# HGRN mixer of a hybrid encoder layer: 64-wide corner products with full 128-column weights, first in the bank, then the 32-wide products of both directions as one group

## The chip, the cores and the metric

The kernel runs on one core of one Trainium2 chip. The metric is the time of one execution on the device in microseconds (us); lower is better. Times given are medians of several executions; a profile is one further execution.

## The reference

One layer of a bidirectional encoder, run on two sequences of 512 and 1024 tokens (12 tiles of 128 tokens, 3 blocks of 512), width 1024, all f32. Each layer norms its input, projects it, and runs two token mixers side by side: a Gated DeltaNet (GDN, 4 heads) and an HGRN2 (4 heads, key and value width 128), each forward and backward. Their outputs are gated, merged and projected, and a SwiGLU feed-forward follows. The part that the change touches is the HGRN2 recurrence, per head and direction:

```
S_t = diag(f_t) S_{t-1} + k_t v_t^T      k_t = 1 - f_t      o_t = S_t^T q_t
cum    = cumsum(logf)                    # inside a chunk
attn   = where(causal, (q * exp(cum)) @ (k * exp(-cum))^T, 0)
o      = attn @ v + (q * exp(cum)) @ S   # S carried from chunk to chunk
S_next = S * exp(cum_last) + (k * exp(cum_last - cum))^T @ v
```

The backward direction is the same on the flipped sequence, and both outputs are added, so one 128 x 128 matrix of scores per tile can hold the forward direction on one side of the diagonal and the backward direction on the other.

## The kernel before, in words

The kernel takes chunks of 128 tokens for the HGRN2. exp(cum) and exp(-cum) over 128 tokens would overflow, so the 128 x 128 scores of a tile are cut by distance from the diagonal, each piece with its own reference point for cum. For one head, one block of 512 tokens (4 tiles, index t) and one direction d, these products are made, all with 128 partitions of contraction (the key width):

- 16 diagonal products of 32 x 32 (4 per tile), from `e1` (queries) and `e2` (keys); forward into the bank `pa`, backward into a second bank `pb`
- 8 products of 32 x 32 (2 per tile) that lie beside the diagonal blocks inside each half of 64, from `l32`
- 4 products of 64 x 64 (1 per tile), the corner between the two halves of 64, from `l64`; forward and backward fill opposite corners of `pa`

`level(w)` prepares `l32` and `l64`: two subtractions on POOL, an exponential on ACT, two multiplications on DVE. `hg_pre` runs this for one direction, then makes its products, transposes the decayed keys `kd` and multiplies them with the values into a state increment. `hg_attn` runs the two directions side by side for each block, then copies `pa` and `pb` out of PSUM under masks that drop what no direction needs, and `hg_mix` carries the state and forms the outputs. There are 4 heads x 3 blocks = 12 such blocks in the program.

All f32 matmuls here run as two passes on TensorE, each with its own weight load. Most of TensorE's work is something else: projections, whose operands are split into a high and a low fp32r part and whose passes move 512 columns (tiles `ha` and `wa`). The GDN mixer has narrow products of its own: merges of 32 x 32 and 64 x 64 pieces, with contraction 32 and 64.

Two planners set the order. `Plan.run` walks five generators (GDN, HGRN, prelude, projections, second phase) by their priority and by estimated times; a `yield pl.at(tile)` hands over until that tile is estimated ready. That gives a program order. `Tape.schedule` then places every instruction on its engine's queue, taking of the instructions that are estimated ready the one that comes first in program order. It adds an estimated 400 ns whenever TensorE goes from one narrow weight shape to another or back, and to keep these few, it ties products of one narrow shape that follow each other in the program into one unit, which is placed whole (`Tape.units`). A product with 128 x 128 weights has no such shape (`o.form` stays None) and is placed alone, between whatever else is ready:

```
                    o.occ = 2 * (2 * k / 2.4 + 5.5) if k > 32 else 35
                    if form != (P, P):
                        o.form = form
```

`k` is the number of moving columns. The estimates only set the order; the chip runs each engine's queue in that order with semaphores.

Of the kernel before, what the change touches and what calls it, by code (L numbers as in the profile page):

```python
# [20 lines left out]
P = 128  # L21
# [671 lines left out]
def layer(ctx, tc, x_p, x_s, w_in, conv_w, a_log, dt_bias, gdn_w, lb_logits, hg_w, w_bg, w_bh,  # L693
# [57 lines left out]
    def mm(out, lhsT, rhs, start=True, stop=True):  # L751
        nc.tensor.matmul(out, lhsT, rhs, start=start, stop=stop)
        n = pl.cols(rhs)
        pl.op("PE", out, [lhsT, rhs], n / 2400.0 if rhs.dtype == F32R else max(0.05, n / 600.0))
# [120 lines left out]
    def t4(ap):  # L875
        return ap.rearrange("p (t c) -> p t c", c=P)
# [125 lines left out]
    def par(*gens):  # L1002
        st = [[0.0, g] for g in gens]
        while st:
            s = min(st, key=lambda c: c[0])
            yield ("at", s[0])
            try:
                r = next(s[1])
            except StopIteration:
                st.remove(s)  # L1010
                continue
            while callable(r):
                yield r
                r = 0
            s[0] = pl.end if r is None else r[1] if isinstance(r, tuple) else 0.0
# [592 lines left out]
    def hg_attn(q, h):  # L1608
        out = q.hg[h]
        for b in range(q.nb):  # L1610
            pa = px()
            pb = px()
            yield from par(*[hg_pre(h, out, b, d, t4(pa), pb[:, 0:P].rearrange("p (t c) -> p t c", c=32))
                             for d in range(2)])
            a_ = ht_("pa", 2)
            av = t4(a_)
            pset(a_, 0.0)
            nc.vector.copy_predicated(av, m_all[:, None, :].to_broadcast([P, 4, P]), t4(pa))
            pl.op("DVE", a_, [pa, a_])
            bd = sblk("bd").rearrange("p (t c) -> p t c", c=32)  # L1620
            pset(bd, 0.0)
            nc.vector.copy_predicated(bd, m_b[:, None, :].to_broadcast([P, 4, 32]),
                                      pb[:, 0:P].rearrange("p (t c) -> p t c", c=32))
            pl.op("DVE", bd, [pb, bd])
            for j in range(4):
                sl = slice(32 * j, 32 * j + 32)
                tt(av[sl, :, sl], av[sl, :, sl], bd[sl], ALU.add)
            out["pa", b] = a_
            yield None

    def hg_pre(h, out, b, d, pav, pbv):
        q = out["q"][b]
        sf = out["sf%d" % d][b]
        vtok = out["v"][b]
        li = d * 4 + h
        lf = blk("lf")
        act(lf, sf, AF.Ln, scale=oml[:, li:li + 1], bias=lb[:, li:li + 1])
# [40 lines left out]
            tt(dm[:, :, q_z], qv[:, :, q_z], dm[:, :, q_z], ALU.mult)  # L1678
            return dl

        def level_mm(w, dl):
            for t in range(4):
                for j in range(P // (2 * w)):
                    o0 = 2 * j * w
                    ks = slice(o0 + k_z * w, o0 + k_z * w + w)
                    qs = slice(o0 + q_z * w, o0 + q_z * w + w)
                    mm(pav[ks, t, qs], t4(dl)[:, t, ks], t4(dl)[:, t, qs])

        l32 = level(32)
        yield pl.at(e1, e2)  # L1690
        for t in range(4):
            for j in range(4):
                sl = slice(32 * j, 32 * j + 32)
                fs = slice(t * P + 32 * j, t * P + 32 * j + 32)
                mm(pav[sl, t, sl] if d == 0 else pbv[sl, t, :], e2[:, fs], e1[:, fs])
        l64 = level(64)
        et = sp.tile([P, 4], F32, name="et", tag="et", bufs=8)
        qs_ = ht_("qd", 4)
        kd = blk("kd")
# [10 lines left out]
            act(t4(kd), c, AF.Exp)  # L1710
        tt(kd, kk, kd, ALU.mult)
        tt(qs_, q, qs_, ALU.mult)
        yield pl.at(l32)
        level_mm(32, l32)
        yield pl.at(l64)
        level_mm(64, l64)
        yield pl.at(kd)
        kdt = blk("kdt")
        transp(kdt, kd)
# [577 lines left out]
```

## Time and profile before

| | us |
|---|---|
| median of 3 runs | 2542.62 (2541.12 to 2545.33) |
| profiled execution | 2537.38 |
| its span, first to last instruction | 2535.7 |
| TensorE (PE) busy | 2481.3 (98%) |
| weight loads (PEld) busy | 2038.3 (80%) |
| VectorE (DVE) busy | 1726.6 (68%) |
| ScalarE (ACT) busy | 1298.2 (51%) |
| GpSimd (POOL) busy | 738.7 (29%) |

Nearly all instructions carry line 577, where the planned order is emitted, so groups are told apart by tiles and shapes. Names of tiles are those of arenas: `ha`, `wa` hold the split operands of projections, `la`, `ba` most f32 tiles of the mixers, `sa` constants such as the identity of a transpose, `bank` PSUM. In a row, `128*64 128x64` means weights of 128 partitions and 64 columns and a result form of 128 x 64; `x8` is the number of passes; a second number after the start is the length. The bracket at the end of a row is the idle time before it and what ended it. PEclk is the clock granted to TensorE, 1.00 being full. The HGRN products run between 116 and 1257 us of the span.

### The profile page before, as it was taken

Reading aid. Unit: us, or ns where it says so; the run is one execution under the profiler, and the core shown is the slowest. Engines: PE = TensorE matmul, PEld = TensorE weight load, DVE = VectorE, ACT = ScalarE, POOL = GpSimd, SP = SyncE. Lnnn points to the kernel's source line nnn. Section 1 sums busy time; section 2 is a strip of 40 time slices with the busy share of each in tenths; the row PEclk is TensorE's granted clock in tenths of the full one; section 3 lists DMA queues with packets and bytes.
Section 4 is the critical chain, followed back from the end, with each engine's and each line's share of the span. In section 5 each row is a group of like instructions: output and inputs, shape, how many; then the busy total and the mean of one; then the engine's idle time right before and its main releaser. Section 6 shows DMA issues by size and latency. Waiting matters only on the chain.

```text
span 2535.7 us, 37670 instructions
## 1 busy us (share of the span) xinstructions
PE 2481.3 (98%) x13992; PEld 2038.3 (80%) x13992; DVE 1726.6 (68%) x2863; ACT 1298.2 (51%) x2202; POOL 738.7 (29%) x1011
## 2 busy tenths in 40 slices
PE   7999999999999999999999999999999999999998
PEld 6778888887878878888888888878888888888886
DVE  5877788768776665775766565664787787734458
ACT  5756666655656555663645435443444344433333
POOL 1551604152322231140100002112567676200014
PEclk9999999999999999999999999999999999999999
DMA  6245352322330331240576553354355455484453
GB/s 160 69 119 134 83 151 72 106 46 64 96 92 22 88 83 30 60 137 30 183 237 224 179 178 112 116 169 140 98 178 187 155 194 187 146 286 127 152 184 137
DMA packets 387303, 330.38 MB, mean 130 GB/s; under 512 B 55241, under 2 KB 315935, under 8 KB 387119
## 3 DMA queue, kind: packets, MB, share of 16 engines
q1 hardware_dynamic: 387119, 327.97, 42.4%
q8 instruction: 110, 1.80, 0.3%
q14 instruction: 74, 0.61, 0.1%
HBM read 251.44 MB, written 76.46 MB: 129 GB/s over the span
## 4 chain that ended last, share of the span: by engine, by line
PE 83%; DVE 6%; DMA 3%; POOL 3%; ACT 2%; issue 2%; SPq 1%; DVEq 0%; POOLq 0%; ACTq 0%
PE bank L577 83%; DVE la_a L577 3%; DVE ba_a L577 2%; POOL sm_a L577 1%; ACT la_a L577 1%; SPq L577 1%; DMA la_a<-dram_cr_sc 1%; POOL ba_a L577 1%; DVE wa_a L577 1%; ACT ba_a L577 1%; POOL la_a L577 1%; DMA la_a<-dram_u_sc 0%; ACT wa_a L577 0%; DMA dram_a_sc<-ba_a 0%; DVE sm_a L577 0%
## 5 line engine op out<-in xcount | busy, mean ns | idle before, releaser
L577 PE MATMUL bank<-ha_a,wa_a 128*128 128x512 f32 x5496 | 1455.0, 405 | 3.6 <-DVE wa_a L577 2.3
L577 PEld LDWEIGHTS bank<-ha_a,wa_a 128*128 128x128 f32 x5496 | 1006.8, 189 | 192.7 <-DVE wa_a L577 7.9
L577 PE MATMUL bank<-xr_a,ha_a 128*128 128x512 f32 x1200 | 318.7, 395 | 0.0
L577 PE MATMUL bank<-xr_a 128*128 128x512 f32 x1386 | 315.7, 389 | 0.0
L577 PEld LDWEIGHTS bank<-xr_a 128*128 128x128 f32 x1386 | 260.1, 188 | 54.1
L577 PEld LDWEIGHTS bank<-xr_a,ha_a 128*128 128x128 f32 x1200 | 225.4, 188 | 53.9
L577 DVE TENSOR_TENSOR wa_a<-la_a,wa_a 128x1024 fp32r<-128x1024 f32 (+1 forms) x152 | 172.9, 1148 | 125.4 <-PE bank L577 94.5
L577 POOL TENSOR_TENSOR ba_a<-ba_a 128x512 f32<-128x512 f32 (+1 forms) x127 | 173.9, 1376 | 269.4 <-DVE ba_a L577 100.6
L577 ACT ACTIVATE la_a<-la_a 128x512 f32<-128x512 f32 (+1 forms) x290 | 182.4, 643 | 60.2 <-DVE la_a L577 41.6
L577 ACT ACTIVATE wa_a<-la_a 128x1024 fp32r<-128x1024 f32 (+1 forms) x152 | 146.3, 973 | 118.5 <-PE bank L577 109.5
L577 POOL TENSOR_TENSOR la_a<-la_a 128x256 f32<-128x256 f32 (+1 forms) x56 | 53.8, 976 | 452.5 <-DVE la_a L577 414.6
L577 ACT ACTIVATE ha_a<-ba_a 128x512 fp32r<-128x512 f32 x135 | 84.6, 629 | 160.1 <-PE bank L577 114.2
L577 ACT ACTIVATE wa_a<-ba_a 128x1024 fp32r<-128x1024 f32 (+1 forms) x106 | 96.7, 921 | 124.7 <-PE bank L577 115.3
L577 PE MATMUL bank<-ha_a 128*128 128x512 f32 x480 | 149.4, 392 | 0.0
L577 DVE TENSOR_TENSOR ha_a<-ba_a,ha_a 128x512 fp32r<-128x512 f32 x135 | 130.7, 972 | 21.9 <-ACT ha_a L577 21.6
L577 DVE TENSOR_TENSOR wa_a<-ba_a,wa_a 128x1024 fp32r<-128x1024 f32 (+1 forms) x106 | 117.2, 1114 | 39.8 <-PE bank L577 31.0
L577 PE MATMUL bank<-wa_a,ha_a 128*128 128x512 f32 x576 | 133.7, 389 | 1.9 <-DVE wa_a L577 1.9
L577 POOL TENSOR_TENSOR sm_a<-la_a 128x126 f32<-128x126 f32 (+37 forms) x155 | 76.3, 492 | 199.4 <-DMA la_a<-dram_u_sc 152.9
L577 DVE TENSOR_TENSOR xr_a<-da_a,xr_a 128x1024 fp32r<-128x1024 f32 (+2 forms) x68 | 77.6, 1157 | 74.5 <-ACT xr_a L577 52.1
L577 ACT ACTIVATE ba_a<-ba_a 128x512 f32<-128x512 f32 (+1 forms) x184 | 115.2, 634 | 25.3 <-DVE ba_a L577 14.0
L577 PEld LDWEIGHTS bank<-wa_a,ha_a 128*128 128x128 f32 x576 | 108.0, 188 | 24.7 <-DVE wa_a L577 2.4
L577 ACT ACTIVATE xr_a<-da_a 128x1024 fp32r<-128x1024 f32 (+2 forms) x68 | 65.3, 978 | 101.9 <-PE bank L577 83.8
(193 smaller groups left out, 3605.0 us busy)
## 6 DMA issues: line engine op xcount, KB each, us to landing
la_a<-w_in SPq DMA_DIRECT2D x77, 512.0 KB
ba_a<-w_ffn_gate SPq DMA_DIRECT2D x36, 512.0 KB
ba_a<-w_ffn_up SPq DMA_DIRECT2D x33, 512.0 KB
dram_a_sc<-xa_a SPq DMA_DIRECT2D x63, 256.0 KB
ba_a<-w_in SPq DMA_DIRECT2D x27, 512.0 KB
da_a<-dram_a_sc SPq DMA_DIRECT2D x25, 512.0 KB
ba_a<-w_ffn_down SPq DMA_DIRECT2D x22, 512.0 KB
la_a<-w_out SPq DMA_DIRECT2D x17, 512.0 KB
```

Source lines behind the costliest of these rows:

```text
L577: f(*[m(a) for a in o.args], **{k: m(a) for k, a in o.kw.items()})
```

## The change

The code of `hg_pre` that made products is moved to `hg_attn`, behind the preparation of both directions; what came after the products becomes `hg_post`. The order in a block is now:

1. prepare both directions: `e1`, `e2`, `l64`, then `l32`, `kd`, `qd`, and wait until all four level tiles are estimated ready
2. the corner products: the full 128 columns of `l64` of a tile as weights, 64 columns of it as moving operand, into all 128 partitions of that half of `pa`. Of each product one half of the partitions is the wanted corner; the other half is written with numbers that nobody needs, and is overwritten by step 3 or dropped by the mask
3. the 48 products of 32 columns of both directions in one stretch of the program
4. both directions' transposes and state increments (`hg_post`), then the masked copies as before

```diff
-            yield from par(*[hg_pre(h, out, b, d, t4(pa), pb[:, 0:P].rearrange("p (t c) -> p t c", c=32))
-                             for d in range(2)])
+            parts = [{}, {}]
+            yield from par(*[hg_pre(h, out, b, d, parts[d]) for d in range(2)])
+            pav, pbv = t4(pa), pb[:, 0:P].rearrange("p (t c) -> p t c", c=32)
+            halves = [slice(0, 64), slice(64, P)]
+            yield pl.at(parts[0]["l64"], parts[1]["l64"], parts[0]["l32"], parts[1]["l32"])
+            for d in range(2):
+                dl = t4(parts[d]["l64"])
+                for t in range(4):
+                    mm(pav[:, t, halves[1 - d]], dl[:, t, :], dl[:, t, halves[1 - d]])
+            for d in range(2):
+                e1, e2, l32 = [parts[d][n] for n in ("e1", "e2", "l32")]
+                for t in range(4):
+                    for j in range(4):
+                        sl = slice(32 * j, 32 * j + 32)
+                        fs = slice(t * P + 32 * j, t * P + 32 * j + 32)
+                        mm(pav[sl, t, sl] if d == 0 else pbv[sl, t, :], e2[:, fs], e1[:, fs])
+                    for j in (0, 2):
+                        ks, qs = [slice(32 * (j + z), 32 * (j + z) + 32) for z in (d, 1 - d)]
+                        mm(pav[ks, t, qs], t4(l32)[:, t, ks], t4(l32)[:, t, qs])
+            yield from par(*[hg_post(out, b, d, parts[d]) for d in range(2)])
...
-        def level_mm(w, dl):
-            for t in range(4):
-                for j in range(P // (2 * w)):
-                    o0 = 2 * j * w
-                    ks = slice(o0 + k_z * w, o0 + k_z * w + w)
-                    qs = slice(o0 + q_z * w, o0 + q_z * w + w)
-                    mm(pav[ks, t, qs], t4(dl)[:, t, ks], t4(dl)[:, t, qs])
-
+        l64 = level(64)
+        yield pl.at(e1, e2)
         l32 = level(32)
-        yield pl.at(e1, e2)
-        for t in range(4):
-            for j in range(4):
...
-        l64 = level(64)
+        yield 0
...
-        yield pl.at(l32)
-        level_mm(32, l32)
-        yield pl.at(l64)
-        level_mm(64, l64)
+        part.update(e1=e1, e2=e2, l32=l32, l64=l64, kd=kd, qs=qs_, et=et)
+
+    def hg_post(out, b, d, part):
+        vtok = out["v"][b]
+        kd, qs_, et = [part[n] for n in ("kd", "qs", "et")]
         yield pl.at(kd)
```

TensorE's queue shows the change at two places. The names are result bank, then arenas of the operands; the shape is that of the result. The first place is a later block, of the second sequence and its second head. Before, it reads:

```order
L577 MATMUL bank_90<-la_a,ba_a 32x32 x16
L577 MATMUL bank_90<-la_a 32x32 x8
L577 MATMUL bank_87<-la_a 32x32 x16
L577 MATMUL bank_90<-ba_a 32x32 x8
L577 MATMUL bank_89<-ha_a,wa_a 128x512
L577 MATMUL bank_91<-ha_a,wa_a 128x512
L577 MATMUL bank_89<-ha_a,wa_a 128x512 x2
L577 MATMUL bank_91<-ha_a,wa_a 128x512 x2
L577 MATMUL bank_90<-la_a 64x64 x4
L577 MATMUL bank_91<-ha_a,wa_a 128x512
L577 MATMUL bank_93<-sa_a,ba_a 128x128
L577 MATMUL bank_90<-la_a 64x64 x4
```

Now, from the end of the corner products on:

```order
L577 MATMUL bank_94<-la_a 128x64 x2
L577 MATMUL bank_90<-sa_a,la_a 128x128
L577 MATMUL bank_89<-sa_a,ba_a 128x128
L577 MATMUL bank_94<-la_a 128x64
L577 MATMUL bank_87<-ha_a,wa_a 128x512
L577 MATMUL bank_94<-la_a 128x64
L577 MATMUL bank_89<-sa_a,ba_a 128x128
L577 MATMUL bank_87<-ha_a,wa_a 128x512
L577 MATMUL bank_94<-la_a 128x64
L577 MATMUL bank_94<-la_a 32x32 x24
L577 MATMUL bank_88<-la_a 32x32 x4
L577 MATMUL bank_94<-la_a 32x32 x2
```

The two groups of four 64x64 products behind the 32-wide ones are gone; the corners (128x64) stand one by one ahead of the 48 products of 32x32, with transposes (sa) and projection passes between them.

The second place is the first block of the program, whose 32-wide products stood in two groups. Before:

```order
L577 MATMUL bank_94<-la_a 32x32 x24
L577 MATMUL bank_89<-ba_a,la_a 32x32 x16
L577 MATMUL bank_88<-ha_a,wa_a 128x512 x3
L577 MATMUL bank_93<-ha_a,wa_a 128x512
L577 MATMUL bank_88<-ha_a,wa_a 128x512
L577 MATMUL bank_93<-ha_a,wa_a 128x512
L577 MATMUL bank_88<-ha_a,wa_a 128x512 x2
L577 MATMUL bank_93<-ha_a,wa_a 128x512
L577 MATMUL bank_88<-ha_a,wa_a 128x512
L577 MATMUL bank_93<-ha_a,wa_a 128x512
L577 MATMUL bank_88<-ha_a,wa_a 128x512 x2
L577 MATMUL bank_94<-ba_a 32x32 x8
```

Now:

```order
L577 MATMUL bank_93<-ha_a,wa_a 128x512 x2
L577 MATMUL bank_94<-ba_a 128x64
L577 MATMUL bank_93<-ha_a,wa_a 128x512
L577 MATMUL bank_94<-ba_a 128x64
L577 MATMUL bank_93<-ha_a,wa_a 128x512 x5
L577 MATMUL bank_94<-la_a 32x32 x24
L577 MATMUL bank_89<-ba_a,la_a 32x32 x4
L577 MATMUL bank_94<-ba_a 32x32 x2
```

The two groups of 40 and 8 products of 32x32 became one of 48; in its second half the two banks alternate, since each tile's diagonal and neighbour products now follow each other.

More of the change, by code (lines that the diff above doesn't have):

```diff
@@ L1629, in hg_attn, with hg_pre @@
             yield None
-    def hg_pre(h, out, b, d, pav, pbv):
+    def hg_pre(h, out, b, d, part):
         q = out["q"][b]
         sf = out["sf%d" % d][b]
-        vtok = out["v"][b]
         li = d * 4 + h
@@ L1679, in level @@
             return dl
-        def level_mm(w, dl):
-            for t in range(4):
-                for j in range(P // (2 * w)):
-                    o0 = 2 * j * w
-                    ks = slice(o0 + k_z * w, o0 + k_z * w + w)
-                    qs = slice(o0 + q_z * w, o0 + q_z * w + w)
-                    mm(pav[ks, t, qs], t4(dl)[:, t, ks], t4(dl)[:, t, qs])
-        l32 = level(32)
-        yield pl.at(e1, e2)
-        for t in range(4):
-            for j in range(4):
-                sl = slice(32 * j, 32 * j + 32)
-                fs = slice(t * P + 32 * j, t * P + 32 * j + 32)
-                mm(pav[sl, t, sl] if d == 0 else pbv[sl, t, :], e2[:, fs], e1[:, fs])
-        l64 = level(64)
+        l64 = level(64)
+        yield pl.at(e1, e2)
+        l32 = level(32)
+        yield 0
         et = sp.tile([P, 4], F32, name="et", tag="et", bufs=8)
```

## The prediction

> **What bounds the kernel now.** I read the page first (busy shares, chain of waits), then the matmul and weight-load groups with shapes kept apart, then stretches of the TensorE timeline.
>
> ```profile
> PE 2481.3 (98%) x13992; PEld 2038.3 (80%) x13992; DVE 1726.6 (68%) x2863; ACT 1298.2 (51%) x2202; POOL 738.7 (29%) x1011
> PE 83%; DVE 6%; DMA 3%; POOL 3%; ACT 2%; issue 2%; SPq 1%; DVEq 0%; POOLq 0%; ACTq 0%
> ```
>
> TensorE is busy for 98% of the span and 83% of the chain, so the time is nearly the sum of what its queue holds, plus its stalls. An f32 matmul is two passes, each with its own weight load. The 64-wide corner products of the HGRN stage, which the change remakes, are these groups:
>
> ```profile
> L577 PE MATMUL bank<-ba_a 128*64 128x64 f32 x104 | 8.8, 228 | 0.0
> L577 PE MATMUL bank<-la_a 128*64 128x64 f32 x88 | 7.5, 228 | 0.0
> ```
>
> 128*64 is a weight block of 64 columns: 104 + 88 = 192 passes, that is 96 corner products, 8 in each of the 12 blocks (4 heads, 3 blocks of 512 tokens). Busy time is no price here, since a group also holds up what stands before and behind it. So I price groups from starts to starts. In the next rows the first column is the start and the second the length, in us. A plain 512-column pass comes from a long run:
>
> ```profile
> 172.09 8.33 PE L577 MATMUL bank<-ha_a,wa_a 128*128 128x512 f32 x36
> 180.26 0.39 PE L577 MATMUL bank<-la_a 128*128 128x128 f32 x2
> ```
>
> (180.26 - 172.09) / 36 = 0.227 us. Now a block whose 32-wide products stand as one group, followed by its two 64-wide groups:
>
> ```profile
> 836.63 1.29 PE L577 MATMUL bank<-ha_a,wa_a 128*128 128x512 f32 x5
> 837.85 0.46 PE L577 MATMUL bank<-la_a,ba_a 128*32 128x32 f32 x32
> 838.13 0.67 PE L577 MATMUL bank<-la_a 128*32 128x32 f32 x46
> ...
> 839.01 1.65 PE L577 MATMUL bank<-ha_a,wa_a 128*128 128x512 f32 x6
> 840.59 0.68 PE L577 MATMUL bank<-la_a 128*64 128x64 f32 x8
> 841.20 0.50 PE L577 MATMUL bank<-ha_a,wa_a 128*128 128x512 f32 x1
> 841.54 0.27 PE L577 MATMUL bank<-sa_a,ba_a 128*128 128x128 f32 x1
> 841.74 0.68 PE L577 MATMUL bank<-la_a 128*64 128x64 f32 x8
> 842.35 0.73 PE L577 MATMUL bank<-ha_a,wa_a 128*128 128x512 f32 x2
> 842.92 0.27 PE L577 MATMUL bank<-sa_a,ba_a 128*128 128x128 f32 x1
> 843.03 0.27 PE L577 MATMUL bank<-sa_a,la_a 128*128 128x128 f32 x1
> 843.05 0.48 PE L577 MATMUL bank<-ha_a,wa_a 128*128 128x512 f32 x1
> ```
>
> The rows with sa_a, which holds the identity, are transposes, 843.03 - 842.92 = 0.11 us each. From 836.63 to 843.05 are 6.42 us with 14 plain passes (3.18) and 3 transposes (0.33): **2.91 us** for the groups of this block. A block whose 32-wide products stand as two groups, with its 64-wide groups later:
>
> ```profile
> 859.29 0.38 PE L577 MATMUL bank<-ba_a 128*128 128x128 f32 x2
> 859.43 0.48 PE L577 MATMUL bank<-ha_a,wa_a 128*128 128x512 f32 x1
> 859.75 0.38 PE L577 MATMUL bank<-ba_a 128*128 128x128 f32 x2
> 859.88 0.48 PE L577 MATMUL bank<-ha_a,wa_a 128*128 128x512 f32 x1
> 860.29 0.72 PE L577 MATMUL bank<-la_a 128*32 128x32 f32 x48
> 860.95 3.48 PE L577 MATMUL bank<-ha_a,wa_a 128*128 128x512 f32 x14
> ...
> 865.10 0.73 PE L577 MATMUL bank<-ha_a,wa_a 128*128 128x512 f32 x2
> ...
> 872.71 1.07 PE L577 MATMUL bank<-ha_a,wa_a 128*128 128x512 f32 x4
> ...
> 876.18 0.49 PE L577 MATMUL bank<-ha_a,wa_a 128*128 128x512 f32 x1
> ```
>
> 859.88 to 865.10 is 5.22, less 15 plain passes (3.41): 1.81 for the two halves. 872.71 to 876.18 is 3.47 with 7 plain passes (1.59), 3 transposes (0.33) and both 64-wide groups: 1.55 for these. So a 64-wide group costs 0.775 us, a whole 32-wide group 2.91 - 1.55 = 1.36, two halves 0.45 more.
>
> **The change part by part.** *Before, summed.* By the order of instructions 7 blocks have one 32-wide group and 5 have two: 7 x 2.91 + 5 x (1.81 + 1.55) = 20.4 + 16.8 = 37.2 us.
>
> *32-wide products in one group.* Twelve groups at 1.36 are 16.3 us. The products are the same 48 in another sequence; inside the group I change nothing.
>
> *Corners with full weights.* The 24 groups of 64-wide weights go (24 x 0.775 = 18.6 us). In their place stand 96 products with 128 weight columns and 64 moving columns, 192 passes, mostly one by one among plain passes. No row of before has this shape, so I bound it. Above: the rows at 859.29 to 859.75 hold one plain pass and one f32 product of 128 weight and 128 moving columns: 0.46 - 0.227 = 0.233 for its two passes, 0.117 a pass. Below: the pace of the 64-wide passes, which stream the same 64 columns. Their eight loads take
>
> ```profile
> 840.59 0.54 PEld L577 LDWEIGHTS bank<-la_a 128*64 128x64 f32 x8 [0.36 <-issue]
> L577 PEld LDWEIGHTS bank<-la_a 128*32 128x32 f32 x608 | 8.5, 112 | 2.4 <-issue 2.0 <-DVE la_a L577 0.4
> L577 PEld LDWEIGHTS bank<-la_a 128*64 128x64 f32 x88 | 5.9, 137 | 3.2 <-issue 2.8 <-POOL sm_a L577 0.4
> L577 PEld LDWEIGHTS bank<-sm_a,la_a 128*128 128x128 f32 x320 | 53.6, 189 | 12.7 <-DVE sm_a L577 2.8 <-ACT sm_a L577 1.3 <-ACT ba_a L577 0.2
> ```
>
> 0.54 us from the first's start to the last's end, one 0.137: (0.54 - 0.137) / 7 = 0.058 a pass. Which end holds depends on whether a pass goes by its moving columns or by its weight columns. The last three rows decide me: a load's length grows by 25 ns from 32 to 64 columns and by 52 ns from 64 to 128, about 0.8 ns a column beside a fixed part, so 128 columns occupy some 0.104 us, twice the 64 columns of streaming. Halving the moving columns then saves nothing while each pass has its own load. I take the upper end: 96 x 0.233 = 22.4 us. At the lower end it is 192 x 0.058 = 11.1.
>
> The Trainium skill (TensorE: Matmul & The Clock Gate, section LDWEIGHTS) has a load cost its columns divided by 1.2 in ns, 107 ns for 128; this rule speaks against the change, and the rows above bear out its slope. By its figure the sum for the corners, an estimate, would be 192 x 0.107 = 20.5 us in place of 22.4.
>
> *Sum.* After: 16.3 + 22.4 = 38.7, against 37.2: **+1.5 us**. At the lower end 16.3 + 11.1 = 27.4: -9.8.
>
> *Waits.* TensorE waits longest in the first of the twelve blocks:
>
> ```profile
> 118.99 2.56 PE L577 MATMUL bank<-ha_a,wa_a 128*128 128x512 f32 x10 [0.66 <-DVE wa_a L577]
> 127.75 0.51 PE L577 MATMUL bank<-wa_a,ra_a 128*128 128x512 f32 x1 [2.37 <-ACT wa_a L577]
> 128.84 0.51 PE L577 MATMUL bank<-wa_a,ra_a 128*128 128x512 f32 x1 [0.48 <-DVE wa_a L577]
> 131.52 0.48 PE L577 MATMUL bank<-sa_a,la_a 128*128 128x128 f32 x1 [0.35 <-DVE la_a L577]
> 110.00:135.00 25.00, 21.13 (x191) 15.73 (x190) 19.98 (x30) 14.99 (x25) 22.20 (x49) 0.93 0.14 45
> 130.40:133.70 3.30, 2.95 (x12) 2.04 (x11) 0.69 (x1) 0.34 (x1) 2.60 (x10) 0.50 0.02 5
> 747.71 3.00 PE L577 MATMUL bank<-ha_a,wa_a 128*128 128x512 f32 x7
> 750.50 0.63 PE L577 MATMUL bank<-la_a 128*128 128x128 f32 x2
> ```
>
> The waits are 0.66 + 2.37 + 0.48 + 0.35 = 3.86 us. In the two windows (busy time of PE, PEld, DVE, ACT, POOL, then the granted clock) POOL is busy for 22.20 of 25 us and the clock falls to 0.50 for a window. The last two rows show such a clock elsewhere: 7 passes in 2.79 us, against 1.59, so 1.2 us lost. In the new order eight corner products and the plain passes between them fill this place, but what TensorE waits for (DVE, ACT) is not sped up. I take half of the 3.86 as gained: -1.9.
>
> *Moves at no cost.* POOL and DVE issue the same numbers of instructions. Level 64 now goes ahead of level 32 on POOL, and the products wait for both levels of both directions. A block's 8 level subtractions there, at
>
> ```profile
> L577 POOL TENSOR_TENSOR la_a<-la_a 128x256 f32<-128x256 f32 (+1 forms) x56 | 53.8, 976 | 452.5 <-DVE la_a L577 414.6
> ```
>
> 0.976 us, are 7.8 us. Queued behind the last of them is the whole block: 32-wide products, transposes of kd, the masked copies, later the mixing. The cover is plain projection passes, which the order still has around every block. If they run out, it is the third rival. No DMA issue is added; SP's queue changes only by where the order falls.
>
> Together 1.5 - 1.9 = -0.4 us. The profiled execution took 2537.38 us (span 2535.7, the rest lies around it), so it would be 2537.0; the median of the three runs, 2542.62, is 5.2 above, and on that scale I predict **2542.2 us**.
>
> **The rivals.** *One: the corners stream at 0.058 a pass* (loads pulled ahead far enough). For it: most corner products in the order have a 512-column pass ahead, under which a load can hide. Against: each product has two loads in a row, only the first can hide there, and the plain pass behind needs its own. Time: 2542.6 - 9.8 - 1.9 = 2531.
>
> The Trainium skill (same page, Part 1, on engine queue depths) lets TensorE pull loads ahead of running matmuls; no row of before shows by how many.
>
> *Two: the new order loses the stalls.* All 3.86 us of the first block go, and the clock stays up in three more places at 1.2 each: 1.5 - 3.9 - 3.6 = -6.0, 2536.6. For it: the slow clock of the first block comes while the small products and the waits keep the array idle, and full-width corners fill it more. Against: the passes at 747.71 stand behind a merge of the Gated DeltaNet, whose narrow products the change does not touch.
>
> *Three, slower: the late start starves TensorE.* With all four levels wanted first, a block's chain is longer; if the plain passes run out, TensorE stops as at 127.75: 2.37 us and a clock window of 1.2, 3.6 together. One such stall with no gain in the first block gives 1.5 + 3.6 = +5.1, the edge of what can be told, two +8.7: 2548 to 2551, say 2549. It decides from the second on. For it: POOL at 22.20 of 25 us in the first block. Against: POOL is busy for 29% over the span.
>
> That the change does not do what it says is out: the order has 43 groups of narrow weights where there were 73, those of the merges included.
>
> **How the numbers follow.** Forecast 0.48; rival one 0.20, two 0.12, three 0.20. A measurement of this kernel tells about 0.2% (5 us) from no change. Faster by more: 0.20 + 0.12 = 0.32; within: 0.48; slower: 0.20. The range 2530 to 2550 takes in the lower end of the corner price and the first starved block, and is otherwise that of a reshuffled order (four clock windows more or fewer are 4.8 us).
>
> **What would show it.** Right: the new 128x64 products with weights 128*128 stand 0.10 to 0.12 us apart from pass to pass; 12 groups of 96 passes of 128*32 at about 1.36 us; no 128*64. Wrong: passes 0.06 apart (rival one); waits over 2 us on la_a ahead of a 128x64 product, with the clock at 0.50 behind them (rival three); a first block without waits and fewer windows (rival two).

## The result: slower by about half a per cent

The changed kernel takes **2551.77 us** (median of 8, 2547.52 to 2556.57); the kernel before took 2542.11 beside it (8, 2536.70 to 2548.16). The ratio of the comparison is 1.005, with a 95% interval of 1.0036 to 1.0063: slower, and above the predicted range. The two medians are 9.7 us apart. The profiled execution took 2551.76 us, its span 2550.0. The account below compares the two profiled executions, whose spans are 14.3 us apart: the one of the change lies at its median, the one of before (2537.38) is 4.7 us below its own. One execution among those behind this document, of experiment e5 below, took 4125.89 us at a mean clock of 0.557 and is left out of its row.

The profile page after, its busy line, the granted clock in 40 slices and the chain:

```profile
PE 2491.0 (98%) x13992; PEld 2056.7 (81%) x13992; DVE 1734.9 (68%) x2863; ACT 1298.8 (51%) x2202; POOL 747.9 (29%) x1011
PEclk9989999999999999998999999999999999999999
PE 86%; DVE 7%; DMA 2%; ACT 2%; issue 1%; POOL 1%; SPq 0%; DVEq 0%; ACTq 0%; POOLq 0%
```

TensorE still bounds the kernel, with the same 13992 passes. The clock row has two slices at 8, where before has none. The matmul groups after, shapes kept apart, show the change done as written: no `128*64` weights are left, and 144 + 48 = 192 passes stand in their place.

```profile
L577 PE MATMUL bank<-la_a 128*128 128x64 f32 x144 | 23.3, 250 | 0.0
L577 PE MATMUL bank<-ba_a 128*128 128x64 f32 x48 | 8.1, 250 | 0.0
```

**Where the time went.** For every pass I took the time from its start to the next pass's start, subtracted what such a pass takes in a long run (0.227 us for a plain pass, 0.112 for one of 128 x 128, nothing for the narrow and corner passes), and added up the rest by stage. Waits are in it, and so is a slow clock. A pass counts to the HGRN products or to the merges of the Gated DeltaNet (GDN) if it is one of theirs or stands within two or three passes of one. Where this border is set moves the split: with 2 to 12 passes counted in, the merges differ by +14.9 to +12.7, the HGRN products by -2.6 to -7.6 and the rest of the mixers by -0.8 to +5.7.

| excess, us | before | after | difference |
|---|---|---|---|
| HGRN products, with their waits | 39.6 | 35.3 | -4.3 |
| GDN merges, with their waits | 72.2 | 86.9 | **+14.7** |
| rest of the mixers | 32.6 | 33.6 | +1.0 |
| first 40 us | 16.0 | 15.9 | -0.1 |
| second phase (after 1335 us) | 15.7 | 19.3 | +3.6 |

These come to +14.9, against 14.3 between the two spans. The products that the change remakes became cheaper. The loss is in products that it doesn't touch: the merges, the 32 x 32 and 64 x 64 products with contraction 32 and 64.

Much of this is the clock. In the trace after, the granted clock is 0.50 for 51.2 us between the first and the last 30 us of the span, in stretches of 3.41 us or multiples of it; in the trace before it is 20.5 us, in six stretches of 3.41. The Trainium skill (TensorE: Matmul & The Clock Gate, Part 1) has the gate judge TensorE in windows of about 3.4 us and grant either half or all of the clock; the stretches agree. What it costs: a merge of one order took 6.7 us more with five such windows than without (e8, below), 1.3 us a window. The merges have nine windows more than before (47.8 against 17.1 us), by this price some 11.7 of their 14.7 us.

The first merge after, in stretches of one window each (the columns are the stretch, its length, the busy time of TensorE with its passes, the granted clock, DMA share and GB/s):

```profile
135.71:139.12 3.41, 3.41 (x19) 1.00 0.29 45
139.13:142.54 3.41, 1.26 (x10) 1.00 0.35 53
142.54:145.95 3.41, 1.93 (x56) 0.50 0.77 208
145.95:149.36 3.41, 3.13 (x49) 0.50 1.05 228
149.37:152.78 3.41, 3.13 (x21) 0.50 1.18 300
152.78:156.19 3.41, 3.41 (x17) 0.50 0.19 48
156.19:159.60 3.41, 3.41 (x28) 1.00 0.00 0
```

and before:

```profile
140.22:143.63 3.41, 3.41 (x22) 1.00 0.33 50
143.65:147.06 3.41, 3.03 (x82) 1.00 0.86 222
147.06:150.47 3.41, 2.52 (x37) 1.00 1.10 260
150.47:153.88 3.41, 3.41 (x31) 1.00 1.17 324
```

After, a window in which TensorE is busy for 1.26 of 3.41 us goes ahead, and four windows at 0.50 follow. The timeline of TensorE after shows why that window is empty, and what the merge is made of:

```profile
140.00 0.39 PE L577 MATMUL bank<-ba_a 128*128 128x128 f32 x2
143.12 1.35 PE L577 MATMUL bank<-la_a 32*32 32x32 f32 x32 [2.73 <-DVE la_a L577]
145.37 0.26 PE L577 MATMUL bank<-la_a,ba_a 32*32 32x32 f32 x1 [0.90 <-DVE ba_a L577]
...
149.44 1.22 PE L577 MATMUL bank<-ha_a,wa_a 128*128 128x512 f32 x2
150.94 1.60 PE L577 MATMUL bank<-la_a 64*64 64x64 f32 x16 [0.28 <-DVE la_a L577]
```

TensorE stands for 2.73 us. It waits for DVE, which waits for the transfer that brings back the inverse that POOL works out for each head, and which the merges put together. The same row of DVE's timeline, after and then before:

```profile
142.62 0.45 DVE L577 STREAM_TRANSPOSE la_a<-la_a 128x256 f32<-128x256 f32 x1 [1.75 <-DMA la_a<-dram_w_sc]
```

```profile
142.40 0.45 DVE L577 STREAM_TRANSPOSE la_a<-la_a 128x256 f32<-128x256 f32 x1 [1.72 <-DMA la_a<-dram_w_sc]
```

The inverse is there at nearly the same time in both: this row ends at 143.07 us after and at 142.85 before, and the first merge can't begin earlier, whatever TensorE does. Before, TensorE still had other passes to make, and came to the merge without a wait:

```profile
143.34 0.38 PE L577 MATMUL bank<-ba_a 128*128 128x128 f32 x2
143.65 0.89 PE L577 MATMUL bank<-la_a 32*32 32x32 f32 x32
```

After, TensorE made its 420th plain pass at 134.6 us, against 139.7 before, and had made 438 by the start of the merge, against 430: it came early, had spent more plain passes, and the next thing in its queue was the merge. Inside the merge it has 2 plain passes, where before had 8. This one merge accounts for +7.0 us. Of the rest, the eighth accounts for +3.7:

```profile
1146.05:1149.46 3.41, 3.41 (x19) 1.00 0.25 89
1149.46:1152.87 3.41, 2.42 (x98) 1.00 0.00 0
1152.88:1156.29 3.41, 3.41 (x24) 0.50 0.02 5
1156.29:1159.70 3.41, 2.62 (x17) 0.50 0.52 154
1159.71:1163.12 3.41, 3.41 (x24) 0.50 0.24 77
1163.12:1166.53 3.41, 2.64 (x16) 0.50 0.00 0
1166.54:1169.95 3.41, 3.41 (x13) 0.50 0.00 0
1169.95:1173.36 3.41, 3.41 (x21) 1.00 0.00 0
```

A window of 98 narrow passes goes ahead, then five at 0.50. Busy time alone does not tell which window is followed by a slow one: the window at 1159.71 reads as full, holds narrow products in part, and is followed by one at 0.50. The +3.6 of the second phase is one further window at 1743 us and small waits; the last 4543 passes, from 1495 us on, stand in the same order as before.

It is not one odd profile. All 8 executions after have a mean clock of 0.986 to 0.990; the executions of before that were timed with the experiments have 0.9925 on average. Within those of before, a clock lower by 0.001 goes with 1.95 us more. By that, an estimate, 0.0044 of clock is 8.6 of the 9.7 us.

### The profile page after: what moved, and what is told of

It is laid out like the page before. It is cut to its first block, busy times and chain, and to the rows that moved or that the text cites. A ratio compares the mean times of both kernels' runs of the same rounds, so it can differ in the third digit from the quotient of the medians.

```text
span 2550.0 us, 37644 instructions
## 1 busy us (share of the span) xinstructions
PE 2491.0 (98%) x13992; PEld 2056.7 (81%) x13992; DVE 1734.9 (68%) x2863; ACT 1298.8 (51%) x2202; POOL 747.9 (29%) x1011
## 4 chain that ended last, share of the span: by engine, by line
PE 86%; DVE 7%; DMA 2%; ACT 2%; issue 1%; POOL 1%; SPq 0%; DVEq 0%; ACTq 0%; POOLq 0%
PE bank L577 86%; DVE la_a L577 3%; DVE ba_a L577 1%; DVE wa_a L577 1%; ACT la_a L577 1%; SPq L577 0%; POOL la_a L577 0%; DVE sm_a L577 0%; ACT ba_a L577 0%; POOL sm_a L577 0%; DMA la_a<-w_in 0%; POOL ba_a L577 0%; DMA dram_a_sc<-ba_a 0%; ACT wa_a L577 0%; DMA la_a<-x_sample 0%
## 5 line engine op out<-in xcount | busy, mean ns | idle before, releaser
L577 ACT ACTIVATE la_a<-la_a 128x512 f32<-128x512 f32 (+1 forms) x318 | 199.8, 647 | 60.4 <-DVE la_a L577 36.5
L577 DVE TENSOR_TENSOR wa_a<-la_a,wa_a 128x1024 fp32r<-128x1024 f32 (+1 forms) x140 | 158.2, 1140 | 83.6 <-PE bank L577 72.9
L577 POOL TENSOR_TENSOR la_a<-la_a 128x256 f32<-128x256 f32 (+1 forms) x67 | 64.4, 981 | 479.1 <-DVE la_a L577 458.6
L577 ACT ACTIVATE wa_a<-ba_a 128x1024 fp32r<-128x1024 f32 (+1 forms) x118 | 109.2, 935 | 153.1 <-PE bank L577 143.3
L577 ACT ACTIVATE wa_a<-la_a 128x1024 fp32r<-128x1024 f32 (+1 forms) x140 | 134.0, 967 | 99.6 <-PE bank L577 90.9
L577 DVE TENSOR_TENSOR wa_a<-ba_a,wa_a 128x1024 fp32r<-128x1024 f32 (+1 forms) x118 | 132.7, 1132 | 58.8 <-PE bank L577 41.9
L577 DVE TENSOR_TENSOR la_a<-la_a 128x512 f32<-128x512 f32 (+3 forms) x215 | 143.1, 684 | 6.9 <-ACT la_a L577 6.0
L577 POOL TENSOR_TENSOR sm_a<-la_a 128x126 f32<-128x126 f32 (+37 forms) x155 | 83.9, 541 | 168.7 <-DMA la_a<-dram_u_sc 157.8
L577 PEld LDWEIGHTS bank<-la_a 128*32 128x32 f32 (+3 forms) x1738 | 108.3, 136 | 30.7 <-DVE la_a L577 10.2
L577 PE MATMUL bank<-la_a 128*32 128x32 f32 (+4 forms) x1738 | 115.8, 222 | 12.5 <-DVE la_a L577 7.5
```

Source lines behind the costliest of these rows:

```text
L577: f(*[m(a) for a in o.args], **{k: m(a) for k, a in o.kw.items()})
```

## The experiments

In the table "excess" is worked out as above, from each run's one profiled execution, whose time is in the column "profiled" and can lie some us off the median (e5 +6.3, e9 -6.4); "half clock" is the time at 0.50 inside the eight merges; the clock is the mean of all timed executions. Ratios are to runs of the kernel before on the same chip, whose medians were 2539.15 us (e1 to e4), 2540.12 (e5 to e8), 2539.52 (e9 to e11) and 2541.18 (e12); the clock of before is that of these runs.

| run | median us | ratio (95%) | profiled | HGRN | merges | half clock | clock |
|---|---|---|---|---|---|---|---|
| before | 2542.11 | 1 | 2537.38 | 39.6 | 72.2 | 17.1 | 0.9925 |
| the change | 2551.77 | 1.0050 (1.0036 to 1.0063) | 2551.76 | 35.3 | 86.9 | 47.8 | 0.988 |
| e1 narrow corners | 2537.33 | 0.9993 (0.9979 to 1.0008) | 2541.09 | 29.9 | 81.8 | 47.8 | 0.991 |
| e2 two groups | 2550.54 | 1.0042 (1.0029 to 1.0055) | 2553.88 | 41.5 | 83.6 | 58.0 | 0.988 |
| e3 estimate | 2549.28 | 1.0043 (1.0028 to 1.0057) | 2547.98 | 37.5 | 81.0 | 44.4 | 0.988 |
| e4 preparation alone | 2546.56 | 1.0024 (1.0010 to 1.0037) | 2545.99 | 42.0 | 74.2 | 23.9 | 0.993 |
| e5 table, change | 2533.74 | 0.9976 (0.9961 to 0.9990) | 2540.03 | 34.8 | 78.8 | 34.1 | 0.994 |
| e8 useless passes | 2543.64 | 1.0012 (0.9996 to 1.0027) | 2542.91 | 35.9 | 77.4 | 41.0 | 0.990 |
| e6 late mark, narrow | 2534.26 | 0.9975 (0.9961 to 0.9989) | 2536.42 | 33.5 | 75.4 | 30.7 | 0.993 |
| e7 table, narrow | 2534.85 | 0.9983 (0.9968 to 0.9998) | 2532.67 | 31.3 | 76.4 | 20.5 | 0.993 |
| e9 table, before | 2546.13 | 1.0025 (1.0009 to 1.0042) | 2539.70 | 38.0 | 75.3 | 23.9 | 0.991 |
| e10 table, narrow | 2534.57 | 0.9983 (0.9967 to 0.9999) | 2533.74 | 30.4 | 75.5 | 23.9 | 0.992 |
| e11 less fill, before | 2540.02 | 1.0008 (0.9995 to 1.0021) | 2539.88 | 49.6 | 72.5 | 23.9 | 0.992 |
| e12 corners twice | 2560.35 | 1.0092 (1.0061 to 1.0124) | 2559.49 | 56.1 | 80.5 | 44.4 | 0.989 |

### The change in parts: e1 to e4

e1 keeps the new order of preparation and the one group of 32-wide products, and makes the corners with 64 weight columns again, behind that group (the loop around this line moves there too):

```diff
-                    mm(pav[:, t, halves[1 - d]], dl[:, t, :], dl[:, t, halves[1 - d]])
+                    mm(pav[halves[d], t, halves[1 - d]], dl[:, t, halves[d]], dl[:, t, halves[1 - d]])
```

> Undoes one part: as the changed kernel (both directions prepared first, one group of 48 32-wide products), but the corners are again products of 64 weight columns, eight in one group behind the 32-wide ones. Theory A (the reordering around the products costs the time: plain passes leave the first block and the GDN merges, whose windows then fall to half clock): the HGRN products cost 12 x (1.36 + about 1.25) = 31 us, 2 to 3 less than the changed kernel, the time at half clock inside the mixer stays well over the 20.5 us of before (30 us or more), and the time is 2540 to 2552, not clearly faster than before. Theory B (the wide corners themselves are dear or pull the clock down): the half-clock time goes back to about 20 us and the time to 2538 or less.

Measured: the same time as before, ratio 0.9993. The median is in theory B's range, the half clock (47.8 us) is what theory A said. Its products are the cheapest of these four, 9.7 us below before and 5.4 below the change. So one group of 32-wide and one of 64-wide products per block is a gain, and corners with 128 weight columns give 5.4 us of it back. But its merges cost 81.8, 9.6 more than before, with the first one at half the clock for 13.65 us here too. What lengthens the merges is thus not the full-width weights alone; it comes with the new order of the preparation and of the products.

e2 keeps the wide corners first and splits the 32-wide group by direction again:

```diff
                         mm(pav[ks, t, qs], t4(l32)[:, t, ks], t4(l32)[:, t, qs])
-            yield from par(*[hg_post(out, b, d, parts[d]) for d in range(2)])
+                yield from hg_post(out, b, d, parts[d])
```

> Undoes the other part: wide corners first, as in the changed kernel, but the 32-wide products of the two directions stand apart, with the first direction's transposes and state increments between them (24 groups of 24 products in place of 12 of 48). By the group price of before (two halves 0.45 us dearer than a whole) the HGRN products cost 12 x 0.45 = 5.4 us more than in the changed kernel. Theory A: on top of that the merges come out otherwise, by up to 6 us either way, 2551 to 2563. Theory B: 2557, since the corners are as dear as before.

Measured: ratio 1.0042. The products cost 6.2 us more than in the change, 0.52 for each of 12 blocks; the prediction had read 0.45 for two halves. The merges stay long at 83.6. The total did not rise with the products: it is that of the change, just below the 2551 from which the expectation started, since the merges and the second phase came out shorter.

e3 is the changed kernel with a longer estimate of a corner pass in the planner, so that only places in the queue change:

```diff
+                    if k == 64 and form == (P, P):
+                        o.occ = 190
```

> The products and their program order are those of the changed kernel; only the planner's estimate of a wide corner product is changed, from 118 to 190 ns (the changed kernel's trace has 170 to 195 for its two passes), so instructions are placed otherwise. Theory A: the HGRN products cost the same within 1 us, but the merges and the half-clock time come out otherwise and the time moves with them, by 3 us or more: 2544 to 2556. Theory B: the time stays at 2552 within 2 us, since the same products are made.

Measured: ratio 1.0043, so a truer estimate does not mend the order. It is 2.5 us below the change with overlapping intervals, which does not decide between the two theories. By placing alone, the same products cost 2.2 us more in the HGRN than in the change and 5.9 less in the merges.

e4 is the kernel before with level 64 prepared ahead of level 32, and its products as they were:

```diff
+        l64 = level(64)
         l32 = level(32)
         yield pl.at(e1, e2)
...
-        l64 = level(64)
```

> The kernel before with one line moved: level 64 is prepared ahead of level 32, and the products keep their shapes and their order in the program. In the order the 32-wide products stand in 30 groups in place of 17, so by the group price they cost 13 x 0.45 = 5.9 us more. Theory A: a mere reordering of the preparation also shifts the merges and the half-clock time by several us: the time is 2548 plus or minus 5, and the half-clock time in the mixer differs from 20.5 us by 6 or more. Theory B: 2548, with the half-clock time as before within one window of 3.4 us.

Measured: ratio 1.0024, slower by some 6 us, although no product and no instruction is added. By the order of instructions it has 30 groups of 32-wide weights where before has 17: the product stage is cut up by the later `l32`. The group price made this 5.9 us, and the HGRN measured +2.4. The rest is spread: merges +2.0, rest of the mixers +2.6. Its mean clock is that of before (0.993), so this loss is not the clock's. To move one line of preparation is not free in this kernel.

### The cover ahead of the merges: e5 and e8

`HOLD` is a table of the planner: how many of the four gate projections of a head may run before the inverse of that head reaches a set step (`MSTEP`); the others are kept back until then, for the merge. e5 is the changed kernel with

```diff
-HOLD = ((2, 2, 2, 1), (2, 2, 2, 2))
+HOLD = ((3, 3, 3, 2), (3, 3, 3, 3))
```

> The changed kernel with one table of the planner changed, which sets how many gate projections wait for the GDN inverse (3 of 4 go free in place of 2, so the projections fall otherwise); products and their shapes are the same. In the order the first GDN merge now has 16 plain and f32 passes between its groups in place of 2. Theory (the slowdown is lost fill: TensorE waits ahead of the first merge, its start being set by POOL's inverse, and the near-idle windows then halve the clock): no or one half-clock window at 140 to 160 us in place of four, merges start at 143 to 145 us as in every kernel so far, and 4 to 7 us less than the changed kernel: 2545 to 2548. Rival (wide corners cost the time wherever they stand): 2552 within 2 us.

e8 is the changed kernel with 16 more plain passes ahead of the first head's wait for the inverse. Their results are never read.

```diff
+        if h == 0 and q.si == 0:
+            fill = px()
+            for k in range(16):
+                mm(fill, ones_r, q.hT[0][k // KD][:, k % KD, :])
         yield ("at", inv_end[0])
```

> The changed kernel with 16 useless plain passes more (ones as weights, result never read) in the program ahead of the first GDN merge, 16 x 0.227 = 3.6 us of TensorE work; the order places them ahead of the first HGRN block, and other projection passes fall later, between the merge's groups. Theory: the merge starts at 143 to 145 us all the same, the 3.0 us wait ahead of it shrinks below 1 us, the half clock of 13.65 us there shrinks to two windows or fewer, and the time is not above the changed kernel's: 2546 to 2552. Rival (TensorE's work is the time): 2555, 3.6 us more.

Measured: e5 2533.74 (ratio 0.9976), 18 us below the change with the same products, faster than before, and 11 us below the range that its theory gave. e8 does 16 x 0.227 = 3.6 us more work than the change and takes 8 us less, also below its range. The same windows of e8:

```profile
141.64:145.05 3.41, 3.41 (x20) 1.00 0.34 53
145.05:148.46 3.41, 2.77 (x74) 1.00 0.58 139
148.46:151.40 2.94, 2.35 (x37) 1.00 1.04 245
151.41:154.82 3.41, 3.12 (x20) 0.50 1.13 307
154.82:158.23 3.41, 3.41 (x22) 0.50 0.43 131
```

The window ahead of the merge is full, the clock stays up for the first two thirds, and the half clock lasts for two windows in place of four. In e5 it lasts for one. That merge's excess falls from 14.0 to 9.9 (e8) and 10.1 us (e5), before's being 7.0. The wait ahead of the merge is down from 2.73 us to 0.03 (e8) and 0.69 (e5).

So cover put back at the first merge takes away the wait and much of the half clock there. But e5 and e8 differ from the change in two things at once: TensorE does not stand ahead of the merge, and nine plain passes stand inside it in place of two. e12 (below) has one without the other. There the first merge begins at 141.57 us without a wait, has 2 plain passes inside, and its windows are:

```profile
138.10:141.51 3.41, 3.41 (x24) 1.00 0.35 54
141.51:144.92 3.41, 2.72 (x88) 1.00 0.73 196
144.93:148.33 3.40, 3.35 (x24) 0.50 1.09 231
148.34:151.75 3.41, 2.55 (x20) 0.50 1.19 293
```

10.24 us at half clock follow, though the window ahead of the merge was full. So the slow clock does not need the stop, which adds its own 2.73 us. What goes with the slow clock in all the kernels of the table is few plain passes inside: the first merges with 1 to 4 of them (the change, e1, e2, e3, e12) have 10.24 to 13.65 us at 0.50, those with 7 to 15 have 0 to 6.83.

The first merge is not the whole gain. In e5 it gives 3.9 of the 18 us, and all the merges give 8.1 in its profiled execution; what gave the rest stays open. In e8 it gives 4.1, the eighth merge 6.7, and the fifth takes some 4 back, with 17.07 us at half clock in place of 6.83.

For the eighth merge the order does not settle it. In e8 the eighth merge has the same order as after (23, 4 and 5 plain passes between its parts), and:

```profile
1145.50:1166.00 20.50, 17.94 (x266) 1.00 0.41 139
```

it ran at the full clock throughout, with an excess of 11.4 us against 18.1 after. In e5 the same merge has this order too, with 10.24 us of half clock and an excess of 15.6. One order, and 0, 10.24 or 17.07 us of half clock: 11.4, 15.6 or 18.1 us, 1.3 to 1.4 for each window. What differs is what stands ahead, and with it how the products fall on the windows; that this is the reason was not tested by itself. The Trainium skill (same page and Part) says that the window runs freely, so that the same kernel has different numbers of matmuls at the slow clock from run to run. The three runs fit this, though they are three kernels.

### Other orders with narrow corners: e6, e7 and e10

All three start from e1. e6 moves the step of the inverse at which the held projections go to a later one; e7 and e10 let more gate projections run ahead.

```diff
-MSTEP = (24, 28)
+MSTEP = (28, 30)
```

> Narrow corners in one group behind one 32-wide group (as in the first experiment), and the planner's mark that lets held gate projections go during the inverse is set later (steps 28 and 30 in place of 24 and 28), so that they fall into the merges: the order has 10 and more passes between the groups of the first merge, and 15 between the later groups of two of the second sequence's. Theory: HGRN products at about 30 us of gap time as in the first experiment, half-clock time in the mixer at 25 us or less against its 47.8, time 2530 to 2537, faster than before. Rival: reordering leaves the time at the first experiment's 2537 to 2541.

```diff
-HOLD = ((2, 2, 2, 1), (2, 2, 2, 2))
+HOLD = ((3, 3, 3, 2), (2, 2, 2, 2))
```

> As the one before, but with the gate table of the first sequence changed (3, 3, 3, 2 in place of 2, 2, 2, 1) and the mark left alone: the first merge has 13 passes between its groups. Theory: no half clock at 140 to 160 us, HGRN products at about 30 us, time 2530 to 2537. Rival: 2537 to 2541.

e10 has e5's table.

> All preparation first and one group of 32-wide products, corners with 64 weight columns, and the table with three projections of gates ahead of the inverse. Theory one: the table repairs the first merge as in the changed kernel (no stretch of half clock of 13 us behind 142 us of the span), and the corners are a few us cheaper than with 128 columns: 2528 to 2533. Rival: the merges fall another way with each order, and the table's worth does not carry over: 2535 to 2545.

Measured: 2534.26, 2534.85 and 2534.57. All three are faster than before, by 0.25%, 0.17% and 0.17%, and their intervals exclude 1, those of e7 and e10 only just (0.9998 and 0.9999, among a dozen orders tried). Their merges are back at 75 to 76 us, and most of the cheaper products stays (30.4 to 33.5 against 39.6). e6 came out in its range of time, but not by the way expected: its half clock, with that of the first HGRN block, is 41.0 us, where 25 or less was expected. e10's first merge has no half clock at all, as expected there, though the time is above the 2533 that I had set. These three and e5 beat both kernels, and are level with each other within their intervals.

### Is it the table or the change: e9 and e11

e9 is the kernel before with e5's table, e11 the kernel before with

```diff
-HOLD = ((2, 2, 2, 1), (2, 2, 2, 2))
+HOLD = ((1, 1, 1, 1), (1, 1, 1, 1))
```

> The kernel before, with the table that lets three in place of two projections of gates per head run ahead of the inverse (the same table made the changed kernel 18 us shorter). Theory one: the changed kernel lost time only because its plain passes ran out ahead of the merges of the Gated DeltaNet; before had enough of them, so the table has nothing to mend here: within 3 us of before, 2537 to 2543, and the excess in the merge stretches stays at 70 to 75 us. Theory two: the table is a gain of its own, whatever the products: 2533 to 2536, and then the faster time of the changed kernel with this table is no merit of the change.

> The kernel before with only one projection of gates per head ahead of the inverse, the other three held back until it is done. No product of the HGRN is touched. Theory one: TensorE runs out of plain passes ahead of the first merges as in the changed kernel; it waits there for 3 us or more, the merges run at the half clock, and the time goes up by 5 to 15 us: 2545 to 2555. Rival: what is held back fills the merges instead, which then hold more plain passes between their narrow products: 2535 to 2542.

Measured: e9 2546.13, ratio 1.0025. Both theories missed: the table is no gain of its own, and it isn't neutral either. So the faster time of e5 belongs to the change with the table, not to the table. Its profile (merges 75.3, as theory one had it) was one of its shorter executions and doesn't show the loss; why before gets slower by it stays open.

e11 came out the same as before, 2540.02, where theory one wanted 2545 to 2555; it is in the rival's range. TensorE did run dry, but earlier, in the first HGRN block:

```profile
119.24 0.45 PE L577 MATMUL bank<-la_a 128*32 128x32 f32 x16
126.92 1.61 PE L577 MATMUL bank<-wa_a,ra_a 128*128 128x512 f32 x2 [7.23 <-ACT wa_a L577]
```

It waited 7.23 us there (HGRN +10), and from then on it was behind, so that the first merge found plain passes in front of it and ran at the full clock (0.0 us at 0.50). The rest of the mixers, with the held projections in it, cost 7.7 less. So the stop cost the HGRN block some 10 us, with 10.24 us at half the clock from 123.4 us on, and later stages gave most of it back. Whether a stop shows in the total thus depends on what comes behind it; which of these stages can give it back was not tested.

### The price of a corner: e12

The disputed price by itself: every wide corner product is made twice, into the same place.

```diff
-                for t in range(4):
+                for t in (0, 0, 1, 1, 2, 2, 3, 3):
                     mm(pav[:, t, halves[1 - d]], dl[:, t, :], dl[:, t, halves[1 - d]])
```

> The changed kernel with each corner product with 128 weight columns made twice, one directly behind the other in the program and into the same place (the second writes what the first wrote, so the result stays the same): 96 more products of two passes. This measures the disputed price. The prediction's price (0.233 us each) adds 22.4 us to the changed kernel, 2574; the price read from the trace after the change (0.17 to 0.20) adds 16 to 19, 2568 to 2571, if the granted clock stays as it was; the prediction's lower end (0.058 a pass) adds 11, 2563. Full-width passes also keep the array busy: if that lifts the clock ahead of the merges, the time comes out lower than the sum, and the products' own stretch has to be read from the profile: passes from start to start at 0.085 to 0.10 there.

Measured: the group rows have 272 + 112 = 384 passes,

```profile
L577 PE MATMUL bank<-la_a 128*128 128x64 f32 x272 | 44.5, 249 | 0.0
L577 PE MATMUL bank<-ba_a 128*128 128x64 f32 x112 | 18.6, 249 | 0.0
```

and the HGRN excess is 56.1 against 35.3: 20.8 us for 96 more products, **0.217 us** each, 0.108 a pass (0.205 to 0.23 each with 2 to 12 neighbouring passes counted in). This is the price of a second product right behind a first. The time rose by less, some 9 us (2560.35 against 2551.77), below the lowest sum of the expectation, since the merges (-6.4) and the second phase (-5.2) came out shorter in this order. The Trainium skill (same page, LDWEIGHTS in Part 2) has a load of 128 columns take 107 ns. By that, an estimate, the two loads of a product take 0.213 us; the run agrees.

## Why the prediction was wrong

**What bounds the kernel**: right. TensorE is at 98% before and after, and its queue and stalls decide.

**32-wide products in one group**: taken at 1.36 us a group. In the trace after, a block reads, with the last corner product and the whole group run together in one row:

```profile
851.41 0.47 PE L577 MATMUL bank<-ha_a,wa_a 128*128 128x512 f32 x1
851.72 1.48 PE L577 MATMUL bank<-la_a 128*128 128x64 f32 x98
853.13 0.33 PE L577 MATMUL bank<-sa_a,ba_a 128*128 128x128 f32 x1
```

853.13 - 851.72 = 1.41 us, less one corner product of 0.2: about 1.2. A little over-priced.

**Corners with full weights**: the upper end of 0.233 was the right one to choose (measured 0.217). It fits the reason given, that the load sets the pace and not the 64 moving columns. Where four passes stand alone they take

```profile
850.14 0.56 PE L577 MATMUL bank<-la_a 128*128 128x64 f32 x4
850.53 0.28 PE L577 MATMUL bank<-sa_a,la_a 128*128 128x128 f32 x1
```

0.39 us, 0.098 a pass. Rival one (0.058 a pass) is out.

**The sum of the products** was +1.5; with the measured prices it is 12 x 1.2 + 96 x 0.217 = 35.2, 2 us below the 37.2 of before, and the whole stage measured -4.3. So the sum was off by some 4 to 6 us, on the side that would have made the kernel faster.

**Waits, -1.9**: in the first block about right, in the total not. The same waits of the first block after:

```profile
118.16 2.35 PE L577 MATMUL bank<-ha_a,wa_a 128*128 128x512 f32 x9 [0.20 <-DVE wa_a L577]
126.73 0.50 PE L577 MATMUL bank<-wa_a,ra_a 128*128 128x512 f32 x1 [0.65 <-ACT wa_a L577]
130.26 0.33 PE L577 MATMUL bank<-sa_a,ba_a 128*128 128x128 f32 x1 [1.47 <-DVE ba_a L577]
```

They are 2.32 us, against 3.86 before: 1.5 gained. TensorE came through the first block some 5 us ahead, and then stood still ahead of the first merge, which can't start before the inverse arrives. In total its waits grew. The waits after, in us, times and longest:

```profile
PE bank L577 <- DVE la_a L577: 16.3, 18, 2.7
PE bank L577 <- DVE ba_a L577: 14.9, 15, 5.3
```

With the shorter lines the sum is 45.9, against 41.3 before.

**Moves at no cost: this step failed.** It said that the cover is "plain projection passes, which the order still has around every block". I asked this of the HGRN blocks and not of the other user of the same cover, the GDN merges, which share one planner and one supply of plain passes. In the trace after, TensorE had made eight more of them by the start of the first merge, stood for 2.73 us ahead of it, and had 2 inside it in place of 8: +7.0 us in this merge, of which e5 and e8 took back some 4 by putting passes there. All eight merges cost +14.7 us, most of it clock. Rivals two and three counted such windows, but two in the wrong direction, and both at one to three windows; the profile has nine more (51.2 against 20.5 us, 3.41 each). The range allowed for four, which is why its upper end of 2550 was passed.

**Rival three** was nearest, with 2549: TensorE stops, and a slow clock follows. Its kind was right, its place and its size were not. It put the stop in the HGRN chain, behind the levels that a block now wants first; TensorE stops for the inverse instead, ahead of products that the change leaves alone, and four windows at half clock came behind the stop, not one. It set the stop at 2.37 and the window at 1.2; the stop was 2.73 and a window 1.3.

**The parts now**, from e1 and the change: one group per width makes the products about 10 us cheaper, full-width corners give some 5 of that back, and the new order costs the merges 10 to 15. Only where the order is mended besides (e5, e6, e7, e10) is something left, 0.17% to 0.25%. What stays open is how much of the loss in the later merges (7.7 of the 14.7 us) is the order and how much the way it falls on the clock's windows: the eighth merge of the change, e5 and e8 shows that one order can have much or none of it.

## What to carry to other kernels

When a planner or a shared queue hands out the filler work, a stage that gets cheaper or earlier takes filler away from another stage: look for the next point that is fixed by another engine (here POOL's inverse), and count the full passes left ahead of it and inside the narrow products behind it. Price a cheaper product only together with the granted clock of its neighbours, window by window, and let the range hold as many clock windows as there are narrow stages. An f32 product of 64 moving columns went here at the pace of its weight loads, 0.098 to 0.108 us a pass with 128 weight columns: to widen its weights from 64 to 128 columns saved no time here, while joining two groups of one width did.

## What the runs showed of the hardware that was not expected

- The half clock came in runs: four and five windows in a row (13.65 and 17.07 us) followed a single one with narrow products or a stop in it; in the trace before there was never more than one in a row. That it holds itself, since narrow products take longer at 0.50 and leave the next window as thin, would fit, and was not tested.
- To add 16 useless full-width passes (3.6 us of work) shortened the changed kernel by 8 us, by the profiles about half of it in the merge that they stand ahead of and the rest in merges far behind.
- The same order of one merge cost 11.4, 15.6 and 18.1 us in three kernels, with 0, 10.24 and 17.07 us at half clock.
- An idle TensorE of 7.23 us in one place (e11) went with no change in the total; one of 2.73 us in another (the change, ahead of the first merge) went with a merge dearer by 7 us. A merge without a stop ahead of it (e12) had 10.24 us at half clock all the same.
